# Sharing the gate products of a routed expert layer out anew between ScalarE and VectorE, and moving the exponential of the gates ahead of the index decoding

## Chip, cores, metric

One core of a Trainium2 chip. The metric is the time of one execution in microseconds on the device; the kernel before took 1887.0 us (median of three runs, 1882.87 to 1887.49).

## What is computed

One layer over 512 tokens of width 1024: a normalised input projection, two mixers (a bidirectional S5 and a bidirectional SSD), their merge, and then the layer that the change lies in, a product-key expert layer, and a final normalisation. Cut to that layer:

```python
q = (xt @ w_q).reshape(t, 8, 2, 128)
scores = einsum('thsd,hskd->thsk', q, sub_keys)            # 8 heads, 2 sides, 128 keys
top_s, top_i = lax.top_k(scores, 16)
cand = top_s[:, :, 0, :, None] + top_s[:, :, 1, None, :]   # 16 x 16 per head
best_s, best_c = lax.top_k(cand.reshape(t, 8, 256), 16)
i1 = take_along_axis(top_i[:, :, 0], best_c // 16, axis=-1)
i2 = take_along_axis(top_i[:, :, 1], best_c % 16, axis=-1)
expert = (i1 * 128 + i2)                                   # 128 of 16384 experts for each token
gates = softmax(best_s)
hid = einsum('td,tkd->tk', x, u_tab[expert])
out = einsum('tk,tkd->td', gelu(hid) * gates, v_tab[expert])
```

## The kernel before

The program is written with a tile framework. Its scheduler fixes the order of the instructions of each engine (and of each engine's DMA queue) when the program is built: among the instructions whose inputs its own model takes to be ready, the one that stands earlier in the program goes first. At run time every engine works its queue in that order and waits by semaphores.

After the mixers (up to about 560 us) come these steps.

*Scores* (`route_scores`): queries by TensorE, scores by TensorE, and VectorE's search for the 16 best of each head and side.

*Pick* (`route_pick(t)`, for each block t of 128 tokens): VectorE adds the candidates (L930, L932), finds the 16 best of each head (`top16`, L915 to L919), and decodes their positions into two indices in a row of dependent operations on one-hot tensors (L943 to L972; the result is `ij`, L956). After it stand the difference of the best scores to the best one (L974, VectorE), its exponential (L975, ScalarE, which loads a table for it), sum, reciprocal and product (L977 to L979). For t = 0 index and gate are kept as they are. For t = 1 to 3 TensorE transposes both indices and the gate (L992, L994) and ScalarE copies the gate into SBUF (L996, `kS`).

*Gates* (`gates(t)`, t = 1 to 3): for each token a matrix of 128 x 128 gate values is built as a product of two one-hot matrices. Eight tokens at a time, here called a half-block (16 in a block of 128 tokens, 48 in all), `onehots` makes `o2` (L1011, VectorE, bf16, with the tokens in pairs innermost), `og`, which is `o2` times the gate (L1015, ScalarE, one token in each activation, four of them; L1016, VectorE, the other four tokens in one operation), and `o1` (L1020, VectorE). TensorE multiplies them token by token (L1034: eight matmuls of fp32, recorded as sixteen passes), ScalarE copies the result to `stg` (L1036, two copies), and for every two half-blocks `stg` is written to `G_d` in memory (L1038). The half-block after the present one is made ahead, and `o2`, `o1` and both halves of `og` have two buffers.

*Dense* (`dense`): for tokens 128 to 511 all 16384 experts are computed, in 128 slices. `up(i)` loads a slice of `u` (L138, 512 KB, SP's queue), splits it (L141, ScalarE, `w_hi`; L142, GpSimd for slices below 34, else VectorE, `w_lo`), makes 24 matmuls (L149 to L151, tile `hid`) and a Gelu (L1052, ScalarE, which needs a table of its own). The first 34 slices stand ahead of the loop over the 128 slices of `v`, whose results are accumulated in PSUM (L1088 to L1090). The accumulators take PSUM that the pick and the gates use, so they start when routing is over; the first 34 slices of `hid` don't need routing and are put between its work. In the program they stand behind it. Tokens 0 to 127 are computed with gathered rows (`gathered`, L1105 to L1127) next to the dense part.

`psm` gives `sm` four buffers in PSUM and `kT` two; `w_hi` and `w_lo` have two buffers and `w_raw` three.

Of the kernel before, what the change touches and what calls it, by code (L numbers as in the profile page):

```python
# [10 lines left out]
F32 = mybir.dt.float32  # L11
# [4 lines left out]
AF = mybir.ActivationFunctionType  # L16
# [71 lines left out]
class Kernel:  # L88
# [832 lines left out]
    def route_pick(self, t):  # L921

        nc, pp = self.nc, self.rp
        V, A, T = nc.vector, nc.scalar, nc.tensor
        sv = self.ts[:, t].rearrange("p (h s) k -> p h s k", s=2)
        cand = pp.tile([128, 8, 50], F32, name="cand", bufs=1)
        off = 0
        for a in range(8):
            n = 16 // (a + 1)
            V.tensor_add(cand[:, :, off:off + n], sv[:, :, 1, 0:n], sv[:, :, 0, a:a + 1].to_broadcast([128, 8, n]))  # L930
            off += n
        V.tensor_add(cand[:, :, off:off + 8], sv[:, :, 0, 8:16], sv[:, :, 1, 0:1].to_broadcast([128, 8, 8]))  # L932
        yield

        best = pp.tile([128, 16, 8], F32, name="best", bufs=1)
        pos = pp.tile([128, 16, 8], U32, name="pos", bufs=1)
        for h in range(8):
            s2 = pp.tile([128, 50], F32, name="cand2", bufs=2)
            self.top16(best[:, :, h], pos[:, :, h], cand[:, h], s2)
        yield  # L940
        bt = lambda n, tag, m=16: pp.tile([128, m, 16, 8], BF16, name=n, tag=tag, bufs=1)
        posb = pp.tile([128, 16, 8], BF16, name="posb", bufs=1)
        V.tensor_copy(posb, pos)  # L943
        idx = pp.tile([128, 2, 16, 8], BF16, name="idxb", bufs=1)
        for sd in range(2):
            V.tensor_copy(idx[:, sd].rearrange("p a h -> p h a"),
                          self.ti[:, t].rearrange("p (h s) a -> p s h a", s=2)[:, sd])
        ij = pp.tile([128, 2, 16, 8], BF16 if t else F32, name="ij", bufs=1)
        st = pp.tile([128, 16, 8], BF16, name="stb", bufs=1)
        over_a = lambda x: x[:, None].to_broadcast([128, 16, 16, 8])  # L950
        over_k = lambda x: x[:, :, None, :].to_broadcast([128, 16, 16, 8])

        def total(x, out):
            for n in (8, 4, 2):
                V.tensor_add(x[:, 0:n], x[:, 0:n], x[:, n:2 * n])  # L955
            V.tensor_add(out, x[:, 0], x[:, 1])  # L956

        ge = bt("ge", "dec", 17)
        V.memset(ge[:, 16], 0.0)
        V.tensor_tensor(ge[:, 0:16], over_a(posb), over_k(self.first), OP.is_ge)  # L960
        oh = bt("oha", "oha")
        V.tensor_sub(oh, ge[:, 0:16], ge[:, 1:17])
        m = bt("ohm", "dec")
        V.tensor_mul(m, oh, over_k(idx[:, 0]))
        total(m, ij[:, 0])
        V.tensor_mul(m, oh, over_k(self.first))
        total(m, st)
        yield
        V.tensor_sub(st, posb, st)
        V.tensor_tensor(oh, over_a(st), over_k(self.count), OP.is_equal)  # L970
        V.tensor_mul(m, oh, over_k(idx[:, 1]))
        total(m, ij[:, 1])  # L972
        gt = pp.tile([128, 16, 8], F32, name="gt", bufs=1)
        V.tensor_sub(gt, best, best[:, 0:1, :].to_broadcast([128, 16, 8]))  # L974
        A.activation(gt, gt, AF.Exp)  # L975
        sm = pp.tile([128, 8], F32, name="gsum", bufs=1)
        V.tensor_reduce(sm, gt.rearrange("p k h -> p h k"), axis=AX.X, op=OP.add)  # L977
        V.reciprocal(sm, sm)
        V.tensor_mul(gt, gt, sm[:, None, :].to_broadcast([128, 16, 8]))  # L979
        gt = gt.rearrange("p k h -> p (k h)")  # L980
        ij = ij.rearrange("p s k h -> p s (k h)")
        if t == 0:
            self.idx0 = self.hp.tile([128, 128], I32, name="idx0")
            self.gt0 = self.hp.tile([128, 128], F32, name="gt0")
            V.scalar_tensor_tensor(self.idx0, ij[:, 0], 128.0, ij[:, 1], op0=OP.mult, op1=OP.add)
            V.tensor_copy(self.gt0, gt)
            return

        kG = self.psm.tile([128, 512], F32, name="kT", tag="mm", bufs=2)
        kT = kG.bitcast(BF16)  # L990
        for i in range(2):
            T.transpose(kT[:, i * 128:(i + 1) * 128], ij[:, i], self.identb)  # L992
        kG = kG[:, 128:256]
        T.transpose(kG, gt, self.ident)  # L994
        kS = pp.tile([128, 128], F32, name="kS", bufs=2)
        A.copy(kS, kG)  # L996
        self.kT[t] = kT, kG, kS
        yield

    def gates(self, t):  # L1000

        nc, pp = self.nc, self.rp
        V, G, A, T = nc.vector, nc.gpsimd, nc.scalar, nc.tensor
        kT, kG, kS = self.kT.pop(t)
        k = lambda s, b: kT[:, s * 128 + 8 * b:s * 128 + 8 * b + 8]

        def onehots(b):

            pairs = [128, 4, 128, 2]
            o2 = pp.tile(pairs, BF16, name="oh2", bufs=2)  # L1010
            V.tensor_tensor(o2, self.col2[:, None].to_broadcast(pairs),  # L1011
                            k(1, b).rearrange("p (a c) -> p a c", c=2)[:, :, None, :].to_broadcast(pairs), OP.is_equal)
            og = [pp.tile([128, 4, 128], F32, name="og", tag=tag, bufs=2) for tag in ("qT", "scr")]
            for j in range(4):
                A.activation(og[0][:, j, :], o2[:, j // 2, :, j % 2], AF.Copy, scale=kS[:, 8 * b + j:8 * b + j + 1])  # L1015
            V.tensor_mul(og[1].rearrange("p (a c) i -> p a i c", c=2), o2[:, 2:4],  # L1016
                         kG[:, 8 * b + 4:8 * b + 8].rearrange("p (a c) -> p a c", c=2)[:, :, None, :]
                         .to_broadcast([128, 2, 128, 2]))
            o1 = pp.tile([128, 8, 128], F32, name="oh1", bufs=2)
            V.tensor_tensor(o1, self.col[:, None, :].to_broadcast([128, 8, 128]),  # L1020
                            k(0, b)[:, :, None].to_broadcast([128, 8, 128]), OP.is_equal)
            return og, o1

        nxt = onehots(0)
        for tb in range(8):
            stg = pp.tile([128, 128, 16], F32, name="stg", bufs=2)
            for q in range(4):
                if q % 2 == 0:
                    og, o1 = nxt
                    if 2 * tb + q // 2 < 15:  # L1030
                        nxt = onehots(2 * tb + q // 2 + 1)
                ps = self.psm.tile([128, 512], F32, name="sm", tag="sm", bufs=4)
                for j in range(4):
                    T.matmul(ps[:, j * 128:(j + 1) * 128], og[q % 2][:, j, :], o1[:, q % 2 * 4 + j, :],  # L1034
                             start=True, stop=True)
                A.copy(stg[:, :, 4 * q:4 * q + 4], ps.rearrange("p (t i) -> p i t", t=4))  # L1036
                yield
            nc.sync.dma_start(self.G_d[(t - 1) * 8 + tb], stg)  # L1038
# [271 lines left out]
```

## Time and profile before

| | |
|---|---|
| median of 3 runs | 1887.0 us (1882.87 to 1887.49) |
| the profiled execution | 1889.53 us |
| its span, first to last instruction | 1887.5 us |
| TensorE busy | 1807.2 us, 96% |
| VectorE busy | 1440.4 us, 76% |
| ScalarE busy | 786.7 us, 42% |
| GpSimd busy | 613.6 us, 33% |
| mean granted clock of TensorE | 0.978 of full speed |

The profile is that of one execution. PE is TensorE's matmul and PEld its weight load, DVE is VectorE, ACT is ScalarE, POOL is GpSimd, SP a queue for DMAs. L1016 is line 1016 of the kernel before. Times are counted from the start of the span. Matmuls overlap, so that the start of one to the start of the next tells what one costs; in the same way operations of VectorE and ScalarE begin some 0.1 us before the one ahead has ended in the record. An idle time that is shown in brackets behind a row is that of the engine just before it, with what ended it.

### The profile page before, as it was taken

The numbers are of one execution on the slowest core, as the hardware profiler recorded it, in microseconds if no ns is written. First come the engines' busy times: TensorE is split into PE (matmuls) and PEld (weight loads), VectorE is DVE, ScalarE is ACT, GpSimd is POOL, SyncE is SP. The second block draws the span as 40 slices with busy tenths as digits, with TensorE's granted clock in tenths as the row PEclk, the third lists the DMA queues.
The fourth block names the chain that finished last, engine by engine and source line by source line (L and its number), as shares of the span: only waits on it lengthen the run. The fifth ranks groups of instructions, "written<-read, shape, count | busy, mean of one in ns | idle before, by whom it ended". The sixth has DMA issues, their size and how long they took to land.

```text
span 1887.5 us, 26535 instructions
## 1 busy us (share of the span) xinstructions
PE 1807.2 (96%) x9351; PEld 1538.1 (81%) x9351; DVE 1440.4 (76%) x2850; ACT 786.7 (42%) x1419; POOL 613.6 (33%) x487
## 2 busy tenths in 40 slices
PE   7999799999999988998999999999999999999998
PEld 3557677777877887898988999999999999998886
DVE  6999956677646799999579777777777777776676
ACT  4235454555322334776633333333333333333333
POOL 1112114444013344222234443434344353343431
PEclk9999999999999998999999999999999999999999
DMA  4322165543632224544699899889989988886675
GB/s 147 106 83 62 49 189 179 150 152 112 234 134 77 96 85 145 202 166 171 251 322 357 315 319 317 295 297 312 311 270 320 310 292 301 313 275 216 245 263 194
DMA packets 174820, 407.40 MB, mean 216 GB/s; under 512 B 20000, under 2 KB 77088, under 8 KB 171616
## 3 DMA queue, kind: packets, MB, share of 16 engines
q1 hardware_dynamic: 129472, 258.27, 40.8%
q0 software_dynamic: 36864, 134.23, 20.1%
q10 hardware_dynamic: 8352, 13.21, 2.0%
q8 instruction: 73, 1.20, 0.3%
q14 instruction: 59, 0.48, 0.1%
HBM read 367.28 MB, written 37.32 MB: 214 GB/s over the span
## 4 chain that ended last, share of the span: by engine, by line
PE 60%; DVE 11%; DMA 2%; issue 2%; POOL 1%; ACT 0%; DVEq 0%; POOLq 0%; ACTq 0%
PE acc L1089 9%; PE acc L1090 9%; PE acc L1088 9%; PE hid L151 7%; PE hid L149 7%; PE hid L150 7%; PE mm L149 3%; PE mm L151 3%; PE mm L150 3%; DVE og L1016 2%; DVE oh L1020 2%; PE sm L1034 2%; DVE ohm L955 1%; DVE oh L1011 1%; DMA G<-G_d 1%
## 5 line engine op out<-in xcount | busy, mean ns | idle before, releaser
L141 ACT CAST w_hi<-w_raw 128x1024 fp32r<-128x1024 f32 (+2 forms) x197 | 198.9, 1011 | 451.6 <-PE hid L150 212.0
L151 PE MATMUL hid<-x2h,w_lo 128*128 128x384 f32 x1024 | 351.5, 343 | 10.7 <-POOL w_lo L142 8.4
L149 PE MATMUL hid<-x2h,w_hi 128*128 128x384 f32 x1024 | 350.6, 342 | 3.5 <-ACT w_hi L141 3.1
L150 PE MATMUL hid<-x2l,w_hi 128*128 128x384 f32 x1024 | 350.3, 342 | 0.0
L142 POOL TENSOR_TENSOR w_lo<-w_raw,w_hi 128x1024 fp32r<-128x1024 f32 (+1 forms) x88 | 200.8, 2284 | 458.5 <-ACT w_hi L141 382.9
L1090 PE MATMUL acc<-vh,Wl 128*128 128x512 f32 x768 | 300.8, 392 | 0.0
L1089 PE MATMUL acc<-vl,Wh 128*128 128x512 f32 x768 | 300.7, 391 | 0.0
L1088 PE MATMUL acc<-vh,Wh 128*128 128x512 f32 x768 | 298.5, 389 | 0.0
L1105 POOL DMA_INDIRECT rowg<-in_u_dram,idx x128 | 194.0, 1516 | 275.4 <-DVE rowg L1117 188.4
L142 DVE TENSOR_TENSOR w_lo<-w_raw,w_hi 128x1024 fp32r<-128x1024 f32 (+1 forms) x109 | 132.7, 1217 | 175.9 <-ACT w_hi L141 175.9
L1105 POOL DMA_INDIRECT rowg<-in_v_dram,idx x128 | 166.1, 1298 | 271.7 <-DVE acc L1127 209.0
L151 PEld LDWEIGHTS hid<-x2h,w_lo 128*128 128x128 f32 x1024 | 196.8, 192 | 12.6 <-POOL w_lo L142 9.7
L149 PEld LDWEIGHTS hid<-x2h,w_hi 128*128 128x128 f32 x1024 | 196.8, 192 | 8.5 <-ACT w_hi L141 4.2
L150 PEld LDWEIGHTS hid<-x2l,w_hi 128*128 128x128 f32 x1024 | 196.5, 192 | 3.7
L154 ACT CAST Wh<-F 128x384 fp32r<-128x384 f32 x128 | 65.9, 515 | 319.1 <-PE acc L1089 279.1
L155 DVE TENSOR_TENSOR vl<-v_raw,vh 128x1024 fp32r<-128x1024 f32 x128 | 158.6, 1239 | 16.6 <-ACT vh L154 15.6
L1090 PEld LDWEIGHTS acc<-vh,Wl 128*128 128x128 f32 x768 | 144.1, 188 | 30.6 <-DVE Wl L155 0.3
L1089 PEld LDWEIGHTS acc<-vl,Wh 128*128 128x128 f32 x768 | 144.1, 188 | 29.0 <-DVE vl L155 0.7
L1088 PEld LDWEIGHTS acc<-vh,Wh 128*128 128x128 f32 x768 | 144.2, 188 | 28.2 <-ACT vh L154 0.4
L1127 DVE SCALAR_TENSOR_TENSOR acc<-rowg,act,acc 128x1024 f32<-128x1024 f32 x127 | 162.4, 1279 | 4.1 <-DMA rowg<-in_v_dram,idx 3.9
L1117 DVE SCALAR_TENSOR_TENSOR rowg<-rowg,xn 128x1024 f32<-128x1024 f32 x128 | 151.9, 1219 | 2.5 <-DMA rowg<-in_u_dram,idx 2.5
L154 ACT CAST vh<-v_raw 128x1024 fp32r<-128x1024 f32 x128 | 134.2, 1048 | 4.9 <-DMA v_raw<-in_v_dram 4.9
(390 smaller groups left out, 3128.7 us busy)
## 6 DMA issues: line engine op xcount, KB each, us to landing
w_raw<-in_ut_dram SPq DMA_DIRECT2D x128, 512.0 KB
v_raw<-in_v_dram SPq DMA_DIRECT2D x128, 512.0 KB
G_d<-stg SPq DMA_DIRECT2D x24, 1024.0 KB
G<-G_d SPq DMA_DIRECT2D x16, 1536.0 KB
w_raw<-in_w_in_dram SPq DMA_DIRECT2D x40, 512.0 KB
RB<-rows_d SPq DMA_DIRECT2D x32, 256.0 KB
w_raw<-in_w_q_dram SPq DMA_DIRECT2D x16, 512.0 KB
E<-rows_d SPq DMA_DIRECT2D x32, 128.0 KB
```

Of the source, the lines that this page charges most:

```text
L141: nc.scalar.copy(hi, raw)
L142: (lo_eng or nc.vector).tensor_sub(lo, raw, hi.bitcast(F32))
L149: mm(ps, ahi(k), bhi(k), start=start and k == 0, stop=False)
L150: mm(ps, ahi(k), blo(k), start=False, stop=False)
L151: mm(ps, alo(k), bhi(k), start=False, stop=stop and k == nk - 1)
L154: self.nc.scalar.copy(hi, src)
L155: (lo_eng or self.nc.vector).tensor_sub(lo, src, hi.bitcast(F32))
L1088: mm(a, wh[:, ts], vh[:, hs], start=k == 0, stop=False)
L1089: mm(a, wh[:, ts], vl[:, hs], start=False, stop=False)
L1090: mm(a, wl[:, ts], vh[:, hs], start=False, stop=k == 127)
L1105: nc.gpsimd.indirect_dma_start(out=r, out_offset=None, in_=tab, in_offset=bass.IndirectOffsetOnAxis(ap=self.idx0[:, k:k + 1], axis=0))
L1127: d = V.scalar_tensor_tensor(self.acc0, r, act[:, k:k + 1], self.acc0, op0=OP.mult, op1=OP.add)
```

## The change

Two edits.

In `route_pick`, the difference of the best scores and its exponential stand directly after the search for the best 16, in front of the decoding, instead of behind it.

In `onehots`, ScalarE makes the products of six of the eight tokens (six activations of 128 x 128) and VectorE those of the last two. VectorE's operation had 512 elements in each partition, and wrote the two tokens of a pair alternately, each element 128 elements from the one before; it now has 256 elements, writes one token after the other in sequence, and reads the one-hot values with a step of two.

```diff
@@ route_pick
             self.top16(best[:, :, h], pos[:, :, h], cand[:, h], s2)
+        gt = pp.tile([128, 16, 8], F32, name="gt", bufs=1)
+        V.tensor_sub(gt, best, best[:, 0:1, :].to_broadcast([128, 16, 8]))
+        A.activation(gt, gt, AF.Exp)
         yield
...
         total(m, ij[:, 1])
-        gt = pp.tile([128, 16, 8], F32, name="gt", bufs=1)
-        V.tensor_sub(gt, best, best[:, 0:1, :].to_broadcast([128, 16, 8]))
-        A.activation(gt, gt, AF.Exp)
         sm = pp.tile([128, 8], F32, name="gsum", bufs=1)
@@ onehots
             og = [pp.tile([128, 4, 128], F32, name="og", tag=tag, bufs=2) for tag in ("qT", "scr")]
-            for j in range(4):
-                A.activation(og[0][:, j, :], o2[:, j // 2, :, j % 2], AF.Copy, scale=kS[:, 8 * b + j:8 * b + j + 1])
-            V.tensor_mul(og[1].rearrange("p (a c) i -> p a i c", c=2), o2[:, 2:4],
-                         kG[:, 8 * b + 4:8 * b + 8].rearrange("p (a c) -> p a c", c=2)[:, :, None, :]
-                         .to_broadcast([128, 2, 128, 2]))
+            for j in range(6):
+                A.activation(og[j // 4][:, j % 4, :], o2[:, j // 2, :, j % 2], AF.Copy,
+                             scale=kS[:, 8 * b + j:8 * b + j + 1])
+            V.tensor_mul(og[1][:, 2:4, :], o2[:, 3].rearrange("p i c -> p c i"),
+                         kG[:, 8 * b + 6:8 * b + 8, None].to_broadcast([128, 2, 128]))
```

## Rows read from the trace of the kernel before

**Rows 1.** The page: busy time of the engines, and shares of the chain that ended last.
```profile
PE 1807.2 (96%) x9351; PEld 1538.1 (81%) x9351; DVE 1440.4 (76%) x2850; ACT 786.7 (42%) x1419; POOL 613.6 (33%) x487
...
PE 60%; DVE 11%; DMA 2%; issue 2%; POOL 1%; ACT 0%; DVEq 0%; POOLq 0%; ACTq 0%
```
**Rows 2.** Busy time of each engine by stretch: one of gates, one of a pick.
```profile
core 0: us, PE busy (x) PEld busy (x) DVE busy (x) ACT busy (x) POOL busy (x), PEclk, DMA share, GB/s
...
740.00:786.00 46.00, 45.15 (x333) 41.45 (x332) 46.00 (x84) 39.22 (x101) 8.72 (x4) 1.00 0.54 207
786.00:808.00 22.00, 18.06 (x95) 17.27 (x94) 22.00 (x64) 8.74 (x14) 7.30 (x4) 0.84 0.29 107
```
**Rows 3.** The same by stretch for instructions of tile hid: PE, PEld, ACT, then PEclk.
```profile
740.00:786.00 46.00, 18.77 (x87) 14.04 (x85) 1.50 (x3) 1.00 0.54 207
786.00:808.00 22.00, 16.90 (x79) 16.10 (x80) 1.52 (x4) 0.84 0.29 107
808.00:853.00 45.00, 18.36 (x85) 13.95 (x85) 1.93 (x4) 1.00 0.53 202
853.00:875.00 22.00, 15.76 (x73) 14.70 (x72) 1.47 (x3) 0.84 0.33 126
875.00:923.00 48.00, 19.82 (x91) 15.06 (x91) 1.96 (x4) 1.00 0.50 193
923.00:955.00 32.00, 29.30 (x156) 28.33 (x156) 2.89 (x6) 0.95 0.79 272
```
**Rows 4.** Timeline in two picks, of t = 0 and t = 3: start, us, engine.
```profile
692.00 0.31 ACT L975 ACTIVATE gt<-gt 128x128 f32<-128x128 f32 x1 [5.38 <-DVE gt L974]
...
855.56 1.28 ACT L975 ACT_TABLE_LOAD   x1
856.00 0.34 PE L149 MATMUL hid<-x2h,w_hi 128*128 128x384 f32 x1
856.52 0.33 PE L149 MATMUL hid<-x2h,w_hi 128*128 128x384 f32 x1
856.85 0.31 ACT L975 ACTIVATE gt<-gt 128x128 f32<-128x128 f32 x1
865.43 0.29 PE L992 MATMUL kT<-identb,ij 128*128 128x128 bf16 x1 [4.38 <-DVE ij L956]
```
**Rows 5.** Timeline of one half-block of the gates, by engine, and TensorE's passes.
```profile
839.44 0.67 DVE L1011 TENSOR_TENSOR oh<-col,kT 128x1024 bf16<-128x1024 bf16 x1
840.03 0.09 DVE L919 MATCH_VALUE_LOAD pos<-best,cand 128x8 f32 x1
840.22 1.06 DVE L1016 TENSOR_TENSOR og<-oh,kT 128x512 f32<-128x512 bf16 x1
841.13 1.20 DVE L1020 TENSOR_TENSOR oh<-col,kT 128x1024 f32<-128x1024 f32 x1
842.26 0.67 DVE L1011 TENSOR_TENSOR oh<-col,kT 128x1024 bf16<-128x1024 bf16 x1
...
840.14 1.28 ACT L1015 ACTIVATE og<-oh,kS 128x128 f32<-128x128 bf16 x4 [0.59 <-DVE oh L1011]
841.33 1.04 ACT L1036 COPY stg<-sm 128x512 f32<-128x512 f32 x2
842.27 0.49 ACT L1052 ACTIVATE F<-hid 128x384 f32<-128x384 f32 x1
842.65 1.04 ACT L141 CAST w_hi<-w_raw 128x1024 fp32r<-128x1024 f32 x1
843.59 1.29 ACT L1015 ACTIVATE og<-oh,kS 128x128 f32<-128x128 bf16 x4
...
850.94 1.86 PEld L1034 LDWEIGHTS sm<-oh,og 128*128 128x128 f32 x16 [0.22 <-ACT stg L1036]
```
**Rows 6.** Groups by line and form, 676 to 930 us.
```profile
L1034 PE MATMUL sm<-oh,og 128*128 128x128 f32 x768 | 97.1, 280 | 2.3 <-DVE oh L1020 1.3
```
**Rows 7.** The stretches of both picks for L1034 alone: PE and PEld busy.
```profile
786.00:808.00 22.00, 1.36 (x13) 1.17 (x11) 0.84 0.29 107
853.00:875.00 22.00, 2.02 (x16) 1.86 (x16) 0.84 0.33 126
```

## Prediction

> **What bounds the kernel now.** I read the page's busy shares and chain first: TensorE is busy 96% of the span and holds 60% of the chain that ended last, VectorE 11% [rows 1]. So the end is set by how much TensorE time is lost, and the question is where it is lost near the change. The table by stretch answers: while tokens 128 to 511 are gated (740 to 786, then 808 to 853 and 875 to 923 us) VectorE is busy all the time, 46.00 of 46 us, and ScalarE 39.22 of 46; while the next 128 tokens are picked (786 to 808, 853 to 875) VectorE is again busy 22 of 22 us and ScalarE only 8.74 [rows 2]. Routing therefore runs at VectorE's pace. TensorE fills the time with the `hid` matmuls of the first 34 expert slices; these must be done anyway before the accumulation starts near 955 us, so a shorter routing gains only the time in which TensorE now stands or runs slowly.
>
> That loss I work out from the `hid` table [rows 3]. One `hid` matmul takes 0.173 us at full clock (three of them from 856.00 to 856.52 [rows 4]); a half-block of eight tokens takes 1.86 us of TensorE for its sixteen passes [rows 5], and 768 passes are 48 half-blocks [rows 6]. From 740 to 955 us, 215 us, the table has 571 `hid` matmuls, 98.8 us, and the 48 half-blocks need 89.3: 26.9 us are lost. In the first pick 79 `hid` need 13.7 us and thirteen late passes of the gates 1.5, loss 6.8 of 22; in the second 73 need 12.6 and sixteen passes 1.9, loss 7.5 [rows 3, 7]. That is 14.3 us in two picks, at a mean granted clock of 0.84 [rows 3]. What it looks like: TensorE waits 4.38 us for the decoded indices (L992 at 865.43) because its queue is in order [rows 4], and the clock stands at the lower of its two levels for a while behind it. The tail (923 to 955) needs 27.0 of 32: 5.0. The three gate stretches keep the rest, 7.6 us, 0.16 per half-block.
>
> **The change, part by part.** *The products on VectorE.* Today one L1016 writes 512 elements, stepped, and holds VectorE from 840.22 to 841.13, 0.91 us [rows 5]. The new one has 256 elements, written in sequence. No row shows it. Lower end: L1020 writes 1024 f32 elements in sequence in 1.13 us (841.13 to 842.26), a quarter is 0.28. Upper end: half of today's stepped write, 0.46. I take 0.35: the rate of L1020, whose write has the same form, with some fixed cost. VectorE's half-block falls from 2.82 us (839.44 to 842.26) to 0.59 (L1011) + 0.35 + 1.13 = 2.07, without the small operation of the next pick that sits in each (0.19, 840.03 to 840.22). Over 48 half-blocks that frees 27 us of VectorE, between 22 and 30.
>
> *The products on ScalarE.* Four hold it from 840.14 to 841.33, 0.30 each; two copies of the result from 841.33 to 842.27, 0.94 [rows 5]. Six and two copies need 1.79 + 0.94 = 2.73 us against 2.13, which is 28.8 us more over 48. On top of it each `hid` slice takes a Gelu (842.27 to 842.65) and a cast (842.65 to 843.59), 1.32 us. So ScalarE, today waiting part of each half-block, becomes the bound of the gates: 48 x 2.73 = 131 us before any `hid` work, where the three stretches last 139 with it. The Trainium skill speaks against the move: "ScalarE: Activation LUTs", Rules for kernel authors, gives multiplication to VectorE, not to ScalarE. The rows agree on price, 0.30 us for a product here against 0.91/4 = 0.23 there; by the rule alone the sum would be 48 x (0.60 - 0.46) = 6.7 us slower, which holds only if the two engines took turns, and they work side by side.
>
> *Difference and exponential ahead of the decoding.* Already today they run there: the exponential, which needs the difference, is at 856.85, and the decoded indices are ready only at 865.43 [rows 4]. The move by itself therefore costs and gains nothing; what covers it is VectorE's decoding. No DMA is in the moved piece, and SP and POOL are passed by nothing; behind it on ScalarE stand Gelus and casts, and for these TensorE waits. Its price shows if that cover goes: the exponential of token block 0 kept ScalarE idle for 5.38 us (the row at 692.00 [rows 4]), since its queue is in order. I put the difference at 0, with ends of -3 and +5 us: 5 is that idle time once more, 3 is part of it removed.
>
> *What goes where.* With VectorE at 2.07 us and ScalarE setting a period of 3.2 (below), VectorE has about 1.1 us free in each half-block, some 18 us in 16 of them, and can do most of the next pick (22 us) inside the gates. I leave 8.5 us of each pick in the open, not 4, as the pick is a chain of dependent operations. Its loss shrinks with it, from 14.3 to 14.3 x 8.5/22 = 5.5: a gain of 8.8 us. Against it, the two exponentials with a table load before and one after (855.56 to 856.85, 1.29 us each [rows 4]) move from an idle ScalarE into a full one: 2 x (2.6 + 0.3) = 5.7 us. The Trainium skill ("ScalarE: Activation LUTs", What ACT_TABLE_LOAD costs) has 2.66 us for a switch with its drain; by that the four loads would cost 10.6 instead of 5.2 us, and 5.4 of the gain below would go. The row shows the exponential 1.29 us behind the start of the load, so I take the row.
>
> *The sum* hangs on one number, the slices k whose `hid` work the planned order puts into the gates; today 263 matmuls [rows 3], 11 slices. The gates last 131 + 5.7 + 1.32k on ScalarE; TensorE's work in them is 89.3 + 4.15k. Their loss is the difference, 47.4 - 2.83k, against 7.6 now. With the 8.8 gained, the time changes by 31.0 - 2.83k. The order now fills TensorE up to 0.16 us in a half-block; if it does so again in the longer half-blocks, k is 14 (156 us of gates, 3.2 us a half-block), and the change is -8.6. I take -7, as part of what is planned will be late. The profiled execution took 1889.5 us (span 1887.5 and 2 around it), 2.5 above the median of the runs; set against the median of 1887.0 that is **1880 us**. Its own range, from a quarter more to half less of the gain and with the move's ends, is 1873 to 1884.
>
> **Rivals.** *ScalarE is full and `hid` starves (slower).* The casts come later in the program than the gates. If the order gives ScalarE to products and copies whenever they are ready, few casts get in, TensorE waits in every half-block for the next products, and the `hid` work is made up after the gates at 4.15 us a slice. Place: the casts of L141 in the gates. Price: 2.83 us for each slice below 11; at k = 9 the time is 5.5 us worse (1893), at k = 6 14 worse (1901), at k = 4 19.7 (1907). For it: ScalarE's load of 2.73 alone nearly fills today's half-block. Against it: today's order does put casts between the copies and products (842.65 [rows 5]). Chance 0.32, mostly at k from 6 to 9.
>
> *One for one (no change).* Gates get slower by what the picks give back: k stays 11 and the sum is 0, or VectorE's free time isn't filled with the pick, the 8.8 us stay lost, and TensorE is kept busy through the longer gates (+1 to -3). About 1887. For it: only one small operation of the next pick stands in each half-block today. Against it: that one was all that VectorE's time allowed. Chance 0.25, with 0.02 in it for the dearer table switch.
>
> *The write doesn't get cheaper by its form.* VectorE's product then takes 0.46 us, its half-block 2.18, still far below ScalarE's 2.73: nothing changes but the overlap of the picks, by 1 to 2 us. It lies inside the forecast's range.
>
> **How the numbers follow.** About 0.3%, 5.7 us, is what a measurement of this kernel can tell from no change. Forecast, faster by more than that: 0.43 (all pick loss and a little of the tail regained gives -18, 1869). Within it: 0.25. Slower: 0.32. Faster and slower share most of the chance, so the range must reach both: 1869 us at the low end and 1904 at the high end, k = 5; beyond lie k below 5 and a gain in other stages.
>
> **What would show it.** Right: the product on VectorE near 0.5 us long from start to end; the one on ScalarE 288 times instead of 192; half-blocks of 3.0 to 3.3 us with TensorE still over 95% busy; picks of 128 tokens mostly inside the gates; the granted clock between the gates above 0.9; accumulation starting near 948 us. Wrong: fewer than 11 slices cast in the gates, TensorE idle before L1034 with ScalarE named, or picks as long as now. A difference that arises before 676 or after 960 us would mean that the order changed elsewhere, and none of my steps has that.

## The result, and the profile after

The changed kernel takes 1903.56 us (median of 6 runs, 1899.39 to 1904.84) against 1887.97 us for the kernel before in the same runs (1882.87 to 1891.34). The ratio is 1.0073, 95% interval 1.0058 to 1.0088: slower by 15.6 us. The forecast was 1880 us and faster; the time lies at the upper end of the range, where the first rival stands. The profiled execution took 1903.67 us, its span is 1901.9 us, 14.4 longer than before.

The page of the changed kernel first: busy time of the engines, and the shares of the chain that ended last.

```profile
PE 1809.2 (95%) x9351; PEld 1548.3 (81%) x9351; DVE 1422.4 (75%) x2850; ACT 811.9 (43%) x1515; POOL 618.2 (33%) x487
...
PE 51%; issue 2%; DMA 1%; POOL 0%; ACT 0%; DVE 0%; DVEq 0%; POOLq 0%; ACTq 0%
```

Against [rows 1] VectorE has lost 18.0 us of work and ScalarE has gained 25.2 us with 96 more instructions (2 x 48 products). The shares of the span hardly move: 76 to 75% and 42 to 43%. These lines say neither that the kernel got slower nor why. Only the page's busy tenths in 40 slices hint at it: in slices 17 to 19 (761 to 903 us) ScalarE goes from 7, 7 and 6 tenths to 9, 8 and 8, and GpSimd from 2, 2 and 2 to 1, 1 and 0. The next view is the timeline of the gates, here of tokens 128 to 255, to hold against [rows 5].

```profile
761.89 1.92 ACT L1015 ACTIVATE og<-oh,kS 128x128 f32<-128x128 bf16 x6
...
763.66 1.10 ACT L1036 COPY stg<-sm 128x512 f32<-128x512 f32 x2
763.82 0.41 DVE L1017 TENSOR_TENSOR og<-oh,kT 128x256 f32<-128x256 bf16 x1
764.15 1.21 DVE L1020 TENSOR_TENSOR oh<-col,kT 128x1024 f32<-128x1024 f32 x1
764.60 1.92 ACT L1015 ACTIVATE og<-oh,kS 128x128 f32<-128x128 bf16 x6
765.28 0.68 DVE L1011 TENSOR_TENSOR oh<-col,kT 128x1024 bf16<-128x1024 bf16 x1
...
765.51 2.02 PE L1034 MATMUL sm<-oh,og 128*128 128x128 f32 x16 [0.71 <-DVE oh L1020]
765.88 1.22 DVE L965 TENSOR_TENSOR oha<-ge 128x2048 bf16<-128x2048 bf16 x1
766.37 1.11 ACT L1036 COPY stg<-sm 128x512 f32<-128x512 f32 x2
...
767.31 1.92 ACT L1015 ACTIVATE og<-oh,kS 128x128 f32<-128x128 bf16 x6
...
768.70 2.02 PE L1034 MATMUL sm<-oh,og 128*128 128x128 f32 x16 [1.17 <-ACT og L1015]
```

Both engines do what the steps said. VectorE's product holds it from 763.82 to 764.15, 0.33 us (before 0.91). ScalarE goes from six products to two copies to six products without a gap, one half-block from 761.89 to 764.60, 2.71 us. In the time that VectorE has left stands work of the next pick (L965, a step of the decoding). But between ScalarE's copies and products there is no Gelu (L1052) and no cast (L141) any more, which [rows 5] still had at 842.27 and 842.65. In the three stretches of gates ScalarE made 11 casts before; now it makes one whole cast there. TensorE therefore has no `hid` to do and stands in front of each half-block: 0.71 us at 765.51, where VectorE's `o1` (L1020) came last, and 1.17 us at 768.70, where ScalarE's products did.

How far that goes is seen in the table by stretch for the instructions of tile `hid`, the same view as [rows 3]. The gates are now 739 to 783, 793 to 838 and 848 to 892 us, the picks between them are 10 us each.

```profile
core 0: us, PE busy (x) PEld busy (x) ACT busy (x), PEclk, DMA share, GB/s
739.00:783.00 44.00, 7.18 (x26) 4.16 (x25) 0.00 (x0) 1.00 0.48 189
783.00:793.00 10.00, 7.53 (x33) 7.29 (x34) 0.87 (x2) 0.83 0.45 170
793.00:838.00 45.00, 3.85 (x17) 2.35 (x15) 0.00 (x0) 1.00 0.44 176
838.00:848.00 10.00, 8.37 (x38) 8.07 (x39) 1.37 (x3) 0.83 0.40 157
848.00:892.00 44.00, 9.17 (x36) 5.69 (x35) 0.79 (x2) 1.00 0.44 180
892.00:973.00 81.00, 74.84 (x407) 73.32 (x408) 7.92 (x17) 0.96 0.84 260
```

In the three stretches of gates stand 26 + 17 + 36 = 79 `hid` matmuls, 3.3 slices; before there were 263, 11 slices. Behind the gates stand 407 where there were 156. Routing ended earlier (the last product at 890.2 instead of 922.7 us), yet the accumulation starts later, at 973.0 instead of 955.0.

The waits from 739 to 892 us (what waited, for what: us in all, times, longest) name the engine:

```profile
POOL w_lo L142 <- ACT w_hi L141: 94.9, 4, 45.8
...
PE sm L1034 <- ACT og L1015: 9.2, 24, 1.2
...
PE hid L149 <- ACT F L1052: 7.0, 2, 4.2
...
PE sm L1034 <- DVE oh L1020: 2.7, 3, 1.2
```

GpSimd, which makes the second half of each split, waits 94.9 of 153 us for ScalarE's casts, at one place 45.8 us in one piece: a whole stretch of gates without a cast. The sum alone is no sign of harm, since GpSimd also waits 136.8 us from 739 to 923 us in the kernel before; there the longest piece is 14.3 us. ScalarE's own queue waits for nothing from 739 to 783 us.

The loss of TensorE, worked out as in the prediction (length of the stretch, less 0.173 us for each `hid` matmul, less 1.86 us for each half-block), shows where the time went. The third column is of a kernel that comes below.

```
us lost         before    after    casts_first
three gates        7.6     30.0       2.8
two picks         14.3      7.7       2.0
tail               5.0     10.6      -0.1
sum               26.9     48.3       4.7
```

For after, 48.3 - 26.9 = 21.4 us more are lost; 14 `hid` matmuls fewer were left when the gates began (2.4 us) and these began 1 us earlier, which makes the 18.0 us of the accumulation's start. Of these the rest of the kernel gives 3.6 back (from the accumulation's start to the end 928.9 us instead of 932.5), and 14.4 stay in the span. (The accumulation is the part from the first L1088 on.)

### The profile page after: what moved, and what is told of

Its sections match the earlier page's. It is cut to its first block, busy times and chain, and to the rows that moved or that the text cites. A ratio compares the mean times of both kernels' runs of the same rounds, so it can differ in the third digit from the quotient of the medians.

```text
span 1901.9 us, 26670 instructions
## 1 busy us (share of the span) xinstructions
PE 1809.2 (95%) x9351; PEld 1548.3 (81%) x9351; DVE 1422.4 (75%) x2850; ACT 811.9 (43%) x1515; POOL 618.2 (33%) x487
## 3 DMA queue, kind: packets, MB, share of 16 engines
q0 software_dynamic: 36864, 134.23, 20.1%
## 4 chain that ended last, share of the span: by engine, by line
PE 51%; issue 2%; DMA 1%; POOL 0%; ACT 0%; DVE 0%; DVEq 0%; POOLq 0%; ACTq 0%
PE acc L1089 9%; PE acc L1090 9%; PE acc L1088 9%; PE hid L151 8%; PE hid L149 8%; PE hid L150 8%; DMA w_raw<-in_ut_dram 1%; POOL w_lo L142 0%; ACT w_hi L141 0%; DVE hfin L1140 0%; DVE fo L1147 0%; ACT L1052 0%; POOL rsf L1144 0%; DVEq L1305 0%; POOLq L1305 0%
## 5 line engine op out<-in xcount | busy, mean ns | idle before, releaser
L141 ACT CAST w_hi<-w_raw 128x1024 fp32r<-128x1024 f32 (+2 forms) x197 | 199.0, 1012 | 474.6 <-PE hid L150 231.1
L142 POOL TENSOR_TENSOR w_lo<-w_raw,w_hi 128x1024 fp32r<-128x1024 f32 (+1 forms) x88 | 202.5, 2304 | 473.6 <-ACT w_hi L141 465.7
L1088 PE MATMUL acc<-vh,Wh 128*128 128x512 f32 x768 | 298.5, 389 | 0.0
L142 DVE TENSOR_TENSOR w_lo<-w_raw,w_hi 128x1024 fp32r<-128x1024 f32 (+1 forms) x109 | 132.7, 1218 | 194.3 <-ACT w_hi L141 194.3
L155 DVE TENSOR_TENSOR vl<-v_raw,vh 128x1024 fp32r<-128x1024 f32 x128 | 157.4, 1229 | 21.1 <-ACT vh L154 20.1
L1088 PEld LDWEIGHTS acc<-vh,Wh 128*128 128x128 f32 x768 | 144.2, 188 | 28.3 <-ACT vh L154 0.4
```

Of the source, the lines that this page charges most:

```text
L141: nc.scalar.copy(hi, raw)
L142: (lo_eng or nc.vector).tensor_sub(lo, raw, hi.bitcast(F32))
L155: (lo_eng or self.nc.vector).tensor_sub(lo, src, hi.bitcast(F32))
L1088: mm(a, wh[:, ts], vh[:, hs], start=k == 0, stop=False)
```

## Experiments

Theory: the 6 to 2 split is right for the engines, and the harm comes from the order of ScalarE's queue, fixed when the program is built. Products and copies stand ahead of the casts and Gelus in the program, and with six products in a half-block one of them is always ready, so that casts and Gelus fall out of the gates. Rivals: ScalarE's time itself is the harm and no order helps; the moved exponential with its table loads is the harm; the split costs nothing and the write's new form does something else.

**The two edits apart.** `exp_only` has the moved difference and exponential with the products as before; `products_only` has the 6 to 2 split with the exponential behind the decoding.

```diff
@@ exp_only (on the kernel before, route_pick)
             self.top16(best[:, :, h], pos[:, :, h], cand[:, h], s2)
+        gt = pp.tile([128, 16, 8], F32, name="gt", bufs=1)
+        V.tensor_sub(gt, best, best[:, 0:1, :].to_broadcast([128, 16, 8]))
+        A.activation(gt, gt, AF.Exp)
         yield
```

(and the same three lines taken out behind the decoding; `products_only` is the changed kernel with these three lines put back there.)

> The move of difference and exponential alone, products as before (four and four, stepped). Theory: nothing, 1885 to 1891 us, since both already run ahead of the decoding. Rival (the move blocks ScalarE's queue): 5 us or more slower, with a longer idle time in front of the exponential than the 5.38 us of before.

Measured: 1889.66 us, ratio 1.0003 (0.9992 to 1.0014).

> The six/two split alone, difference and exponential where they stood before. Theory (the products fill ScalarE and the casts and Gelus of the first 34 slices find no place in its order): the whole slowing is here, 1900 to 1905 us, half-blocks of 2.7 us, fewer than 60 hid matmuls in the three gate stretches. Rival (the exponential with its two table loads, now in a full ScalarE queue, is what costs): most of the 15 us goes, 1892 us or less.

Measured: 1902.47 us, ratio 1.0072 (1.0048 to 1.0096). The 6 to 2 edit alone carries the whole loss and the move of the exponential carries nothing. In the trace of `products_only` 169 `hid` matmuls stand between the first and the last product of the gates and the accumulation starts at 972.2 us; with `exp_only` it is 395 and 959.3, and before it was 395 and 955.0. Counted in each stretch from its first to its last product alone, `products_only` has 80 `hid` matmuls, where fewer than 60 were expected, against 66 in the changed kernel and 215 before.

**The write's form alone.** `unstepped4` leaves four tokens to each engine and only lets VectorE write its 512 elements in sequence.

```diff
@@ unstepped4 (on the kernel before, onehots)
-            V.tensor_mul(og[1].rearrange("p (a c) i -> p a i c", c=2), o2[:, 2:4],
-                         kG[...].rearrange("p (a c) -> p a c", c=2)[:, :, None, :].to_broadcast([128, 2, 128, 2]))
+            V.tensor_mul(og[1].rearrange("p (a c) i -> p a c i", c=2), o2[:, 2:4].rearrange("p a i c -> p a c i"),
+                         kG[...].rearrange("p (a c) -> p a c", c=2)[:, :, :, None].to_broadcast([128, 2, 2, 128]))
```

> Four products on ScalarE and four on VectorE as before, but VectorE's one operation writes token after token in sequence (512 elements). Theory: the stepped write is what makes it dear; from start to start it falls from 0.91 to about 0.62 us, VectorE no longer sets the half-block, TensorE does at 2.7 us, and the casts keep their place: 1880 to 1885 us. Rival 1 (the form of the write is free, the operands cost): still about 0.9 us and 1887. Rival 2 (ScalarE is the next bound at once): 2.8 us half-blocks, with ScalarE named in front of L1034, and 1887.

Measured: 1882.75 us, ratio 0.9967 (0.9954 to 0.998). The timeline of `unstepped4`, VectorE in the gates:

```profile
762.36 0.69 DVE L1016 TENSOR_TENSOR og<-oh,kT 128x512 f32<-128x512 bf16 x1
762.97 1.21 DVE L1020 TENSOR_TENSOR oh<-col,kT 128x1024 f32<-128x1024 f32 x1
```

The product holds VectorE for 0.61 us instead of 0.91 [rows 5]: the same 512 products cost a third less when they are written in sequence and the one-hot values are read with a step of two, instead of the other way round. This part of the change is a gain by itself, 6 us, and it takes nothing from ScalarE: 395 `hid` matmuls stay between the first and the last product, and the accumulation starts at 948.5 us.

**The order alone.** `casts_first` is the changed kernel, with the load, the split and the Gelu of the 34 early slices given a high priority when the scheduler orders the instructions. No instruction is added or taken away.

```diff
@@ casts_first (on the changed kernel, up)
-            uh, ul = self.wload(I["ut"][i], 8, 128, lo_eng=G if i < NF else V)
+            first = tc.high_priority(100000) if i < NF else nullcontext()
+            with first:
+                uh, ul = self.wload(I["ut"][i], 8, 128, lo_eng=G if i < NF else V)
...
-            A.activation(f.rearrange("p b t -> p (b t)"), ps, AF.Gelu)
+            with tc.high_priority(100000) if i < NF else nullcontext():
+                A.activation(f.rearrange("p b t -> p (b t)"), ps, AF.Gelu)
```

> The changed kernel, with load, split and Gelu of the first 34 slices given the first place in the planned order wherever they are ready. No work is added or taken away. Theory (the order starves the hid work; ScalarE's load itself would have been borne): the hid matmuls in the gates come back to 260 or more, half-blocks grow to 3.0 to 3.3 us, TensorE is over 95% busy in them, and the time falls from 1903 to 1878 to 1889 us. Rival (ScalarE is simply too full with six products): 1897 us or more, whatever the order.

Measured: 1870.63 us (4 runs, 1868.79 to 1875.22), ratio 0.9914 (0.9887 to 0.9941), 33 us below the changed kernel and 18 below the kernel before, and 7 us below what was expected. ScalarE's time alone is thus not the harm. ScalarE's timeline in the gates of `casts_first` shows what the priority does: a cast and a Gelu go in between three products and the next three.

```profile
868.85 1.06 ACT L1036 COPY stg<-sm 128x512 f32<-128x512 f32 x2
869.79 1.01 ACT L1015 ACTIVATE og<-oh,kS 128x128 f32<-128x128 bf16 x3
870.74 1.05 ACT L141 CAST w_hi<-w_raw 128x1024 fp32r<-128x1024 f32 x1
871.69 0.49 ACT L1055 ACTIVATE F<-hid 128x384 f32<-128x384 f32 x1
872.07 0.98 ACT L1015 ACTIVATE og<-oh,kS 128x128 f32<-128x128 bf16 x3
```

The table by stretch of `casts_first` for tile `hid` (columns as above):

```profile
739.00:787.00 48.00, 25.24 (x106) 17.79 (x106) 2.43 (x5) 1.00 0.48 187
787.00:797.00 10.00, 7.53 (x39) 6.81 (x40) 0.49 (x1) 1.00 0.70 263
797.00:851.00 54.00, 31.57 (x127) 21.28 (x126) 2.94 (x6) 1.00 0.53 195
851.00:858.00 7.00, 6.76 (x39) 6.52 (x38) 0.49 (x1) 1.00 0.59 228
858.00:909.00 51.00, 32.96 (x128) 21.54 (x127) 2.43 (x5) 1.00 0.55 206
909.00:930.00 21.00, 21.00 (x122) 20.74 (x120) 2.41 (x5) 1.00 0.93 326
```

The gates are longer than in the changed kernel, 48 + 54 + 51 = 153 us instead of 133, since ScalarE does more in them. In exchange they hold 106 + 127 + 128 = 361 `hid` matmuls, 15 slices, with 16 casts. The picks in the open are 10 and 7 us, and the clock stays at full speed (2.4 GHz) in both, where it was granted at 0.84 before. TensorE's waits from 739 to 909 us are small:

```profile
PE sm L1034 <- DVE oh L1020: 1.5, 2, 1.0
...
PE sm L1034 <- ACT stg L1036: 1.4, 1, 1.4
...
PEld L992 <- DVE ij L959: 1.1, 1, 1.1
```

The accumulation starts at 929.7 us. Of the 25.3 us won there, 4.5 are lost again behind it (span 1866.7, and 1866.7 - 929.7 = 937.0 instead of 932.5). In the first 145 us behind the accumulation's start TensorE waits 6.0 us for halves that VectorE makes (3.8 for `w_lo`, L142, and 2.2 for `vl`, L155), against 2.3 in the kernel before and none in the changed one. From 930 to 1000 us the DMA engines are busy all the time (share 1.02) in this kernel; whether that makes VectorE late was not tried.

**Is it the order as such, or the order under a full ScalarE?** `before_first` and `unstepped4_first` have the same priorities on the kernel before and on `unstepped4`. `splits_first` and `gelu_first` are the changed kernel with only the first or only the second part of the priority.

> The kernel before (four and four, stepped) with load, split and Gelu of the first 34 slices given the first place. Theory (the first place only undoes the starving that six products bring; with four, ScalarE has gaps and nothing starves): no change, 1884 to 1891 us. Rival (the first place is a gain of its own, and six and two add nothing to it): 1875 us or less, as casts_first had 1870.6.

Measured: 1890.23 us, ratio 0.9997 (0.9982 to 1.0013).

> Four and four with VectorE's write in sequence, plus the first place for the 34 slices. Theory: as without it, 1878 to 1886 us (unstepped4 had 1882.8), because the gates' order is already full of hid matmuls; so the 12 us that casts_first has on it come from VectorE's time freed by six and two and filled with the next pick. Rival: 1873 us or less, so that six and two isn't needed.

Measured: 1882.05 us, ratio 0.9959 (0.9942 to 0.9975), the same as `unstepped4` without it. With four products the priority puts hardly more `hid` into the gates: both kernels keep 398 matmuls between the first and the last product, where each had 395. It is not without effect there. The accumulation starts 5.0 and 5.3 us earlier (950.0 instead of 955.0 us, and 943.2 instead of 948.5), and 7.1 and 5.1 us are lost again behind that start, where TensorE waits 6.7 and 6.4 us for VectorE's `w_lo`. In sum nothing is won. So the 33 us are no gain that this priority brings to any split; with six products it gives back the `hid` work that the full ScalarE had pushed out.

> The changed kernel with the first place for load and split of the 34 slices, but not for their Gelu. Which of the two starves the hid work: if the casts alone, the time falls to about 1872 us; if the Gelu too (hid has two buffers in PSUM, and a third slice waits until a Gelu has emptied one), it stays at 1898 to 1906 us with fewer than 60 hid matmuls in the gates.

Measured, one execution: 1913.52 us, with 118 `hid` matmuls between the first and the last product.

> The changed kernel with the first place for the Gelu of the 34 slices alone. If the casts starve by themselves, the time stays at 1899 to 1906 us; if the Gelu was the whole cause, it falls to about 1872 us.

Measured, one execution: 1908.25 us, with 145. Neither half does it, and both are slower than the changed kernel. In `splits_first` TensorE waits for Gelus (F, L1054: 47.7 us in the whole trace, 16.4 in the changed kernel) and GpSimd 48.8 us for the end of `hid` matmuls; in `gelu_first` TensorE waits for casts (L141: 20.4 us, 12.4 in the changed kernel). A slice needs both of ScalarE's steps; the waits fit that the one that stays behind holds the other. The priority of the load was not separated from that of the split.

**How much per slice.** `first20` gives the priority to slices 0 to 19 alone (`i < 20` in both places).

> A smaller dose: the changed kernel with the first place for load, split and Gelu of the slices 0 to 19 only, so that 20 to 33 starve as before. In the planned order 265 hid matmuls then stand between the first and the last product of TensorE, against 145 in the changed kernel and 427 in casts_first. Theory (what costs is the hid work missing there, matmul by matmul): in a straight line between those two, 33 us for 282 matmuls, so 1903 - 0.117 x 120 = 1889 us, between 1884 and 1894. Rival (the first place helps in some other way, at the first slices or after the gates): near 1871 or near 1903.

Measured: 1889.45 us, ratio 1.0005 (0.9993 to 1.0017). Three kernels that differ in the order alone lie on a line:

```
                hid matmuls between first       median us
                and last product
after                 145                        1903.56
first20               265                        1889.45
casts_first           427                        1870.63
```

From the two ends, 32.9 us by 282 matmuls is 0.117 us for one, 2.80 us for a slice of 24; the line gives 1889.6 for 265. That is the clearest evidence for the theory, as the middle point was forecast from the ends before it ran. Two things stand behind the line. At the accumulation's start (973.0, 955.8 and 929.7 us) a matmul is worth more, 0.14 us in the first step and 0.16 in the second, near the 0.173 that it takes; from there to the end the first two need 928.9 us and `casts_first` 937.0. And the number of matmuls is not all: `gelu_first` and `splits_first`, one execution each, also differ in the order alone and lie 4.7 and 6.8 us above the line. Their last product comes at 894.3 and 898.5 us, in the changed kernel at 890.2.

**A split in the middle.** `five_first` gives ScalarE five tokens and VectorE three, with the priorities of `casts_first`. VectorE does its three in two operations.

```diff
@@ five_first (on casts_first, onehots)
-            for j in range(6):
+            for j in range(5):
...
+            V.tensor_scalar(og[1][:, 1, :], o2[:, 2, :, 1], kS[:, 8*b+5:8*b+6], None, op0=OP.mult)
```

> Five products on ScalarE and three on VectorE (one alone, two in one sequential write), with the first place for the 34 slices. If six and two was right, because VectorE's time was the scarce one, it lies between unstepped4_first (1882) and casts_first (1870.6): 1873 to 1880 us. Rival (six and two had made ScalarE too full): below 1869 us.

Measured: 1883.11 us, ratio 0.9966 (0.9954 to 0.9978): a miss, no better than four to four. The groups of `five_first` in the gates:

```profile
L1017 DVE TENSOR_SCALAR og<-oh,kS 128x128 f32<-128x128 bf16 x48 | 23.1, 481 | 3.0 <-PE sm L1035 1.7
...
L1018 DVE TENSOR_TENSOR og<-oh,kT 128x256 f32<-128x256 bf16 x48 | 19.8, 412 | 0.0
```

In the record VectorE is busy 23.1 + 19.8 = 42.9 us with three tokens in two operations, against 48 x 0.687 = 33.0 us for four in one (the median of L1016 in `unstepped4`) and 20.1 for two in the changed kernel. It is not relieved, and the picks stay in the open (TensorE waits 8.9 us in three pieces for the indices of L959). But the price of a second operation is not the whole of it. 11 of the 48 single products, each beside a GpSimd L142, took from 0.35 to 2.24 us, where the median is 0.286: 9.5 of the 23.1 us are such extra time (see the last section). The other 37 hold VectorE 0.20 us from start to start and the pair 0.33, together 0.53, which is less than the 0.60 for four tokens in `unstepped4`. The expectation had no term for what the single product waits for. From the last product of one block to the first of the next pass 23 us, as in `unstepped4`, where `casts_first` has 11; how much of that comes from these waits and how much from the planned order was not separated.

**The exponential in the good order.** `late_exp_first` is `casts_first` with the three lines of the exponential back behind the decoding.

> casts_first with difference and exponential put back behind the decoding. Theory (the move does nothing by itself): as casts_first, 1866 to 1875 us. Rival (with ScalarE full, the move matters): off by 5 us or more.

Measured: 1870.32 us, ratio 0.9908 (0.9883 to 0.9934). Also here the move is worth nothing.

The best version is thus the 6 to 2 split with the early slices' load, split and Gelu put first, 1870.6 us with either place of the exponential. It beats the kernel before (1888.8 beside it) and the changed kernel.

## Why the prediction went wrong, step by step

**What bounds the kernel, and that a shorter routing pays only through TensorE's lost time:** right in the main. That the accumulation's start moves with the lost time is bookkeeping, since the loss table ends there (for `casts_first` 4.7 - 26.9, less 1.7 for ten `hid` matmuls and 1 for the earlier beginning, is -24.9; measured -25.3). What the runs add is that most of it reaches the end: 14.4 of 18.0 us in the changed kernel, 20.8 of 25.3 in `casts_first`. The prediction had no term for the rest.

**The products on VectorE,** 0.35 us from between 0.28 and 0.46: measured 0.33. The rival that the write doesn't get cheaper falls; `unstepped4` shows the same for 512 elements.

**The products on ScalarE,** 2.73 us a half-block: measured 2.71, and three gates of 133 us against 48 x 2.71 = 130. ScalarE became the bound, as said. All instructions of both products in the changed kernel, with shortest, median and longest duration in ns:

```profile
L1015 ACT ACTIVATE og<-oh,kS x288: 384/430/513, 737.5 to 889.0; 128x128 f32<-128x128 bf16 x144
...
L1017 DVE TENSOR_TENSOR og<-oh,kT x48: 400/420/558, 737.6 to 885.1; 128x256 f32<-128x256 bf16 x48
```

A product costs 1.77/6 = 0.295 us on ScalarE (761.89 to 763.66) and 0.33/2 = 0.165 on VectorE. The rule of the Trainium skill ("ScalarE: Activation LUTs", Rules for kernel authors), that multiplication belongs on VectorE, agrees with these prices. The times don't follow it: with the early slices put first, six to two takes 1870.6 us and four to four 1882.1. The dearer engine was the one with room.

**The picks,** 8.5 us each in the open: measured 10 and 10, and 10 and 7 in `casts_first`. Their loss was to be 5.5 us; it was 7.7 and 2.0. Of these two kernels only `casts_first` had the clock above 0.9 there (1.00). In the changed kernel it is 0.83, and the timeline around 785 us shows why the picks stayed slow:

```profile
772.92 1.28 ACT L942 ACT_TABLE_LOAD   x1
774.21 0.31 ACT L942 ACTIVATE gt<-gt 128x128 f32<-128x128 f32 x1
...
783.63 1.28 ACT L1052 ACT_TABLE_LOAD   x1
...
785.47 0.50 PE L149 MATMUL hid<-x2h,w_hi 128*128 128x384 f32 x1 [2.78 <-ACT F L1052]
...
786.09 0.52 PE L151 MATMUL hid<-x2h,w_lo 128*128 128x384 f32 x1
786.41 0.52 PE L149 MATMUL hid<-x2h,w_hi 128*128 128x384 f32 x1
```

TensorE comes into the pick without work, stands 2.78 us for a Gelu that had to wait for the gates' end, and its next matmuls follow each other at 0.32 us instead of 0.173, the lower of the two levels (1.2 GHz).

**The exponential,** difference 0 between -3 and +5: measured 0 twice. The price of 5.7 us for its table loads in a full ScalarE was too high. In the changed kernel two of the four loads fell into the gates (772.92 above, and 835.14), in `casts_first` none. The exponential follows its load by 1.29 us (772.92 to 774.21) in the full queue too; the 2.66 us of the Trainium skill ("ScalarE: Activation LUTs", What ACT_TABLE_LOAD costs) don't show here either.

**k = 14: this is the step that failed.** "The order now fills TensorE up to 0.16 us in a half-block; if it does so again in the longer half-blocks, k is 14". It didn't: k is 3.3, and the first rival came true beyond its own "k from 6 to 9". The same rule of order that kept TensorE full with four products starves it with six. Why it did so before is inferred, not shown, as no run has the scheduler's own model: ScalarE had waits for VectorE, which [rows 5] show (0.59 us in front of the products at 840.14), and in such gaps a cast, later in the program, can be the only instruction ready. With 2.71 us of products and copies on ScalarE against about 2.1 on VectorE there are no such gaps. The prediction had all of it in hand, the place of the casts in the program and the new ratio of the two engines, and put the tie to TensorE's good; "against it: today's order does put casts between" took the result of those gaps for a rule. The runs that show it are `casts_first`, where the order alone changes and k is 15 (forecast 14) with 153 us of gates (forecast 156), `first20` on the line between, and `before_first`, where the same priority adds hardly any `hid` to the gates while ScalarE still has its gaps.

**The sum,** 31.0 - 2.83k, comes out some 6 us too high at both ends, and that it comes so near is luck. At k = 3.3 it gives +21.7 and the medians differ by +15.6; at k = 15 it gives -11.5 and measured is -18.2. Its parts are further off. In the changed kernel the gates lost 30.0 us instead of 47.4 - 2.83 x 3.3 = 38.1; the picks lost 7.7 instead of 5.5, and the tail 10.6 where the prediction left it at 5.0. These errors cancel, and the lost time rises by 21.4, almost the sum's 21.7; what makes it 14.4 in the span are the 3.4 us won before the table of the gates begins and the 3.6 that come back behind the accumulation's start. In `casts_first` gates, picks and tail lost 2.8, 2.0 and -0.1 us instead of 5.0, 5.5 and 5.0. That none of its table loads stood in the gates can explain no more than the gates' 2.2; the tail and the picks are the larger part. The slope is luck too: the gates alone give (30.0 - 2.8)/11.75 = 2.3 us for a slice, and the measured 2.80 has the tail, the picks and the loss behind the accumulation's start in it. The tail, which shrinks when the early slices are done in time, had no term in k. The forecast's own range, 1873 to 1884, was also added wrongly: half of the gain and the 5 us of the move give 1888 at the upper end.

## What to carry to other kernels

When work moves to an engine with a low share of busy time, look at what else that engine feeds to the bottleneck, and by what rule its queue is ordered: work that the fixed order had let in so far (11 casts in the gates here) can be pushed out (to one), and the share of busy time over the whole span (42 to 43%) doesn't show it; a table by stretch does. Look also behind the stretch that was won: two of the kernels here started the accumulation 5 us earlier with the priority and were not faster. Before a split between engines is judged, the feeding work should be put first and the split timed again: the same 6 to 2 split is 0.7% slower in one order and 0.9% faster in the other. And a part of an edit can be the gain by itself, as the unstepped write (0.3%) was.

## What the runs showed of the hardware that was not expected

An operation of VectorE with all operands in SBUF was held while GpSimd's L142 ran; operations that read `kT`, which lies in PSUM, were not. Timeline of the changed kernel, VectorE and GpSimd:

```profile
785.61 0.68 DVE L958 TENSOR_TENSOR ohm<-ohm 128x1024 bf16<-128x1024 bf16 x1
...
786.81 2.38 POOL L142 TENSOR_TENSOR w_lo<-w_raw,w_hi 128x1024 fp32r<-128x1024 f32 x1 [42.84 <-ACT w_hi L141]
786.87 2.47 DVE L958 TENSOR_TENSOR ohm<-ohm 128x256 bf16<-128x256 bf16 x1
```

With GpSimd idle 1024 elements take 0.68 us; with GpSimd's operation beside it 256 elements take 2.47 us, where others of this size take 0.28 (at 777.33), and end 0.15 us after it. In `casts_first`, beside the same operation of GpSimd:

```profile
860.30 2.38 POOL L142 TENSOR_TENSOR w_lo<-w_raw,w_hi 128x1024 fp32r<-128x1024 f32 x1 [2.26 <-ACT w_hi L141]
...
860.53 0.42 DVE L1017 TENSOR_TENSOR og<-oh,kT 128x256 f32<-128x256 bf16 x1
...
862.00 0.68 DVE L1011 TENSOR_TENSOR oh<-col,kT 128x1024 bf16<-128x1024 bf16 x1
```

Both have their usual length. The place of the operands is not the whole rule. In `five_first`, beside one L142:

```profile
739.93 2.37 POOL L142 TENSOR_TENSOR w_lo<-w_raw,w_hi 128x1024 fp32r<-128x1024 f32 x1 [2.04 <-ACT w_hi L141]
...
740.03 0.18 DVE L917 MATCH_REPLACE8 cand<-best,cand 128x50 f32<-128x50 f32 x1
...
740.14 2.24 DVE L1017 TENSOR_SCALAR og<-oh,kS 128x128 f32<-128x128 bf16 x1
```

The search step (L917) has all its operands in SBUF and is not held; the product behind it, which reads its factor from `kS` in SBUF, takes 2.24 us, where the median is 0.286. 11 of its 48 were held like that, which is a part of the miss of `five_first`. Which resource the two engines share was not tried.
